# Half-size tiles for weight blocks that are split alone, and three raw weight tiles in place of four

## The chip, the cores and the metric

The kernel runs on one core of a Trainium2 chip. The metric is the device time of one execution in microseconds (us); the time before is the median of 3 runs. The engines are TensorE (PE; its weight loads are PEld), VectorE (DVE), ScalarE (ACT), GpSimd (POOL) and SyncE (SP), which here issues nearly all loads.

## The reference

Two decoder layers on 256 tokens of width 2048, in float32. Each layer has a token mixer (HGRN2 in the first, gated linear attention in the second) that shares an input projection with a cross-attention into 256 memory tokens, an output projection, and a SwiGLU feed-forward of width 5632:

```python
    for layer in range(DEPTH):
        hn = _rmsnorm(h, norm_mix[layer])
        ...
        h = h + jnp.concatenate([y, xa], axis=-1) @ w_out[layer]

        hn = _rmsnorm(h, norm_ffn[layer])
        gate, up = jnp.split(hn @ w_gate_up[layer], 2, axis=-1)
        h = h + (jax.nn.silu(gate) * up) @ w_down[layer]
    return _rmsnorm(h, norm_final)
```

What is left out computes y, the mixer's output, and xa, the cross-attention's. Each weight is read once, so the kernel is a stream of weight tiles through the products.

## The kernel before

**Split weights.** Each float32 operand is taken apart into a high part, rounded to the matmul's fp32r format, and a low part, the rest; a product is then three matmuls: high by high, high by low, low by high. For the weights this happens as they come. A load (on SP's queue, L216 and L341) brings a raw tile of four 128 x 512 blocks, 1 MB. `split` takes one or two blocks of it: ScalarE casts them to the high part (L207) and VectorE subtracts to get the low part (L208); both go into one tile called `parts`. TensorE reads the parts.

**The rings.** Raw tiles come from a ring of four, parts from a ring of six, each with room for two blocks, high and low. A load waits until the last split has read the raw tile whose place it takes; a cast waits until TensorE is done with the parts tile whose place it takes. A few other tiles (`side`: keys and values of the memory, a small decay table) sit in the ring of parts for a while.

**Two ways to multiply.** `project` (mixers, w_out, w_down; L249 to L251) splits a raw tile into two parts tiles and makes 24 matmuls of it. `project_halves` (the gate and up product; L333 to L335) saves products by combining blocks. One raw tile holds two blocks of gate and two of up, comes by two loads of 512 KB (the first brings the block that a splits), and is of one of three kinds:

- O: two splits of two blocks (a, b), 24 matmuls.
- H: as O, then one difference (L366) and a split of one block alone (c), 24 matmuls.
- S: a split of one block alone (a), a split of two (b), then three differences written over the raw tile (L350 on two blocks, L351, L352), then two splits of two (c, d), 21 matmuls. L351 needs L350, L352 needs L351, c needs L350, d needs L352.

So an S tile takes four parts tiles, one of them half full; an H tile takes three, one of them half full.

**The feed-forward's blocks.** Each layer has 11 blocks of 512 columns. A block takes eight gate and up tiles, of kinds SHOSHOSO, SHOSSOSO, SHOSSOSO, and from the fourth block (number 3) on SSOSSOSS; then VectorE and ScalarE combine the eight products into the silu-gated result (L830 to L836), TensorE transposes it (L160, with L148 and L149), and pieces of w_down follow between the blocks: four raw tiles per block from block 3 on, with L414 adding the result to the residual. Blocks 3 to 10 are called steady here. Raw tiles are numbered through: 148 to 155 are the gate and up tiles of block 6 of the first layer (kinds S, S, O, S, S, O, S, S), 156 to 159 the w_down tiles behind them.

**What sets the order.** Nothing in the code fixes the order on an engine. A scheduler takes the instructions in the code's order of priority and places each when its inputs and a free slot of its ring are expected; engines then run their lists strictly in order and wait by semaphores. So ring sizes decide not only who waits, but also the lists.

Of the kernel before, what the change touches and what calls it, by code (L numbers as in the profile page):

```python
# [9 lines left out]
F32 = mybir.dt.float32  # L10
F32R = mybir.dt.float32r
# [6 lines left out]
P = 128  # L18
# [17 lines left out]
def trunk_kernel(ctx: ExitStack, tc: tile.TileContext, x, mem, norm_mix, norm_ffn, norm_mem,  # L36
# [5 lines left out]
    wts = ctx.enter_context(tc.tile_pool(name="wts", bufs=1))  # L42
# [153 lines left out]
    def new_raw():  # L196
        i = n_w[0]
        n_w[0] += 1
        return i, wts.tile([P, 4, 512], F32, tag="raw", name=f"raw{i}", bufs=4)

    def split(src, name, by=2):

        n, m = src.shape[1:]
        both = wts.tile([P, 2, 2, 512], F32R, tag="parts", name=f"parts{name}", bufs=6)
        for k in range(0, n, by):
            j = min(k + by, n)
            nc.scalar.copy(out=both[:, 0, k:j, 0:m], in_=src[:, k:j, :])  # L207
            nc.vector.tensor_tensor(out=both[:, 1, k:j, 0:m], in0=src[:, k:j, :],  # L208
                                    in1=both[:, 0, k:j, 0:m].bitcast(F32), op=ALU.subtract)
        return [(both[:, 0, k, 0:m], both[:, 1, k, 0:m]) for k in range(n)]  # L210

    def weights(w, k0, nk, c0, n):
        i, raw = new_raw()
        m = 1 if i == 0 else nk
        for j in range(0, nk, m):
            nc.sync.dma_start(out=raw[:, j:j + m, 0:n],  # L216
                              in_=w[(k0 + j) * P:(k0 + j + m) * P, c0:c0 + n].rearrange("(k p) c -> p k c", p=P))
        return [p for k in range(0, nk, 2) for p in split(raw[:, k:k + 2, 0:n], f"{i}_{k}", 1 if i == 0 else 2)]
# [102 lines left out]
    def project_halves(forms, kinds, w, c0, c1, name):  # L321
# [14 lines left out]

        for p, kind in enumerate(kinds):
            i, raw = new_raw()

            for j, c in ((slice(0, 4, 3), c0), (slice(1, 3), c1)):  # L340
# [4 lines left out]
            if kind == "S":  # L345
                tt = nc.vector.tensor_tensor
                b00, = split(raw[:, 0:1, :], f"{i}a")
                b11, b10 = split(raw[:, 2:4, :], f"{i}b")

                tt(out=raw[:, 0:2, :], in0=raw[:, 0:4:2, :], in1=raw[:, 1:2, :].broadcast_to([P, 2, 512]), op=ALU.subtract)  # L350
                tt(out=raw[:, 2, :], in0=raw[:, 2, :], in1=raw[:, 0, :], op=ALU.add)  # L351
                tt(out=raw[:, 3, :], in0=raw[:, 3, :], in1=raw[:, 2, :], op=ALU.subtract)  # L352
                t5, t7 = split(raw[:, 0:2, :], f"{i}c")
                t6, t4 = split(raw[:, 2:4, :], f"{i}d")
                todo = {1: ("x00", b00), 2: ("x01", b10), 3: ("z", b11), 4: ("x11", t4), 5: ("s", t5), 6: ("u", t6),
                        7: ("d0", t7)}
                for b in (1, 2, 6, 7, 5, 4, 3) if last else (1, 3, 2, 5, 7, 6, 4):
                    product(b, x(todo[b][0]), todo[b][1])
            else:
                b00, b01 = split(raw[:, 0:2, :], f"{i}a")  # L360
                b11, b10 = split(raw[:, 2:4, :], f"{i}b")
                todo = [[(2, "x00", b00), (5, "x10", b01), (4, "x10", b00), (3, "d0", b01)]]
                if kind == "O":
                    todo.append([(2, "x01", b10), (5, "x11", b11), (4, "x11", b10), (3, "d1", b11)])
                else:
                    nc.vector.tensor_tensor(out=raw[:, 3, :], in0=raw[:, 3, :], in1=raw[:, 2, :], op=ALU.subtract)  # L366
                    e1, = split(raw[:, 3:4, :], f"{i}c")
                    todo.append([(2, "x01", b10), (3, "x01", b11), (7, "x11", b11), (4, "x11", e1)])
                todo = [m for ms in zip(*todo) for m in ms] if last else todo[0] + todo[1]
                for b, f, right in todo:  # L370
                    product(b, x(f), right)
# [586 lines left out]
```

## Time and profile before

| | |
|---|---|
| time, median of 3 runs | 2323.41 us (2322.97 to 2323.65) |
| the profiled execution: time, span | 2322.12 us, 2320.3 us |
| TensorE's granted clock | 0.998 |
| read from memory | 430.48 MB, 187 GB/s over the span |
| blocks 3 to 10, first layer | about 675 to 1170 us |
| blocks 3 to 10, second layer | about 1740 to 2240 us |

How to read the rows that follow: a page line gives busy time, share of the span and instructions per engine. A row of windows has the stretch, its length, then busy time and count of PE, PEld, DVE, ACT and POOL, the granted clock, the share of DMA, and GB/s. A row of the timeline has start, duration, engine, line, operation, output from inputs, shapes, and in brackets how long the engine stood idle ahead of it and what ended that. A matmul's duration reaches into the next one's, since they are pipelined: the distance of starts is what counts, and the same holds, less so, for VectorE and ScalarE. A row of DMA issues has tiles, queue, count, KB of one and the median time from issue to landing.

### The profile page before, as it was taken

The numbers are of one execution on the slowest core, as the hardware profiler recorded it, in microseconds if no ns is written. First come the engines' busy times: TensorE is split into PE (matmuls) and PEld (weight loads), VectorE is DVE, ScalarE is ACT, GpSimd is POOL, SyncE is SP. The second block draws the span as 40 slices with busy tenths as digits, with TensorE's granted clock in tenths as the row PEclk, the third lists the DMA queues.
The fourth block names the chain that finished last, engine by engine and source line by source line (L and its number), as shares of the span: only waits on it lengthen the run. The fifth ranks groups of instructions, "written<-read, shape, count | busy, mean of one in ns | idle before, by whom it ended". The sixth has DMA issues, their size and how long they took to land.

```text
span 2320.3 us, 28901 instructions
## 1 busy us (share of the span) xinstructions
PE 2297.6 (99%) x11034; PEld 1934.7 (83%) x11034; DVE 1887.7 (81%) x2262; ACT 1261.2 (54%) x1643; POOL 22.2 (1%) x39
## 2 busy tenths in 40 slices
PE   9999999999999999999999999999999999999998
PEld 7888888888887888888889999988887888888886
DVE  5566565668999999999985665567999999999995
ACT  7543534455555555555555654455555555555563
POOL 0000000000000000000000000000000000000000
PEclk9999999999999999999999999999999999999999
DMA  8554545455556556566565445555555556656563
GB/s 316 192 172 162 164 150 176 145 182 176 186 188 212 200 188 205 189 209 208 183 226 167 150 150 167 161 199 164 178 203 198 201 187 210 202 189 210 200 217 127
DMA packets 229211, 435.51 MB, mean 188 GB/s; under 512 B 10028, under 2 KB 38992, under 8 KB 228816
## 3 DMA queue, kind: packets, MB, share of 16 engines
q1 hardware_dynamic: 227776, 429.40, 55.5%
q10 hardware_dynamic: 1296, 4.26, 0.5%
q8 instruction: 86, 1.41, 0.2%
q14 instruction: 53, 0.43, 0.1%
HBM read 430.48 MB, written 3.15 MB: 187 GB/s over the span
## 4 chain that ended last, share of the span: by engine, by line
PE 63%; DVE 25%; issue 6%; ACT 4%; DMA 0%; ACTq 0%; DVEq 0%; POOLq 0%; SPq 0%
PE f_p L334 5%; PE f_p L335 5%; PE f_p L333 4%; DVE raw L350 4%; DVE parts L208 4%; PE fd L250 3%; PE fd L249 3%; PE fd L251 3%; PE wo L251 3%; PE wo L249 3%; PE wo L250 3%; DVE raw L351 2%; DVE raw L352 2%; PE hgate L249 1%; PE gv L249 1%
## 5 line engine op out<-in xcount | busy, mean ns | idle before, releaser
L208 DVE TENSOR_TENSOR parts<-raw,parts 128x1024 fp32r<-128x1024 f32 (+3 forms) x490 | 557.7, 1147 | 289.1 <-ACT parts L207 288.2
L207 ACT CAST parts<-raw 128x1024 fp32r<-128x1024 f32 (+3 forms) x490 | 476.8, 991 | 424.6 <-PE wo L251 64.4
L350 DVE TENSOR_TENSOR raw<-raw 128x1024 f32<-128x1024 f32 x118 | 143.6, 1217 | 0.2
L351 DVE TENSOR_TENSOR raw<-raw 128x512 f32<-128x512 f32 x118 | 81.6, 692 | 3.9
L352 DVE TENSOR_TENSOR raw<-raw 128x512 f32<-128x512 f32 x118 | 81.6, 692 | 3.8
L414 DVE TENSOR_TENSOR h<-fd,h 128x512 f32<-128x512 f32 x94 | 61.9, 684 | 6.2 <-PE fd L251 6.1
L833 DVE TENSOR_TENSOR e<-f_p,e 128x512 f32<-128x512 f32 x66 | 44.9, 680 | 0.0
L835 ACT ACTIVATE s<-s,rf_r 128x512 f32<-128x512 f32 x44 | 31.8, 722 | 6.9 <-DVE s L833 6.9
L836 DVE SCALAR_TENSOR_TENSOR s<-e,rf_r,s 128x512 f32<-128x512 f32 x44 | 32.3, 742 | 0.0
L562 DVE COPY_PREDICATED sch<-mask,slh 96x512 f32<-96x512 uint8 (+3 forms) x15 | 10.8, 721 | 25.1 <-PE slh L578 25.1
L833 DVE TENSOR_TENSOR s<-f_p,e 128x512 f32<-128x512 f32 x44 | 29.5, 682 | 0.0
L578 PEld LDWEIGHTS slh<-Q,K 128*96 128x96 f32 (+3 forms) x240 | 25.4, 176 | 1.4
L249 PE MATMUL wo<-parts,y_3h 128*128 128x512 f32 x64 | 25.9, 405 | 0.0
L249 PE MATMUL wo<-parts,y_0h 128*128 128x512 f32 x64 | 25.7, 402 | 0.0
L250 PE MATMUL fd<-parts,s_3h 128*128 128x512 f32 x64 | 25.4, 396 | 0.0
L249 PE MATMUL fd<-parts,s_0h 128*128 128x512 f32 x64 | 25.3, 396 | 0.0
L249 PE MATMUL fd<-parts,s_2h 128*128 128x512 f32 x64 | 25.3, 396 | 0.0
L249 PE MATMUL fd<-parts,s_6h 128*128 128x512 f32 x64 | 25.3, 396 | 0.0
L249 PE MATMUL fd<-parts,s_4h 128*128 128x512 f32 x64 | 25.3, 396 | 0.0
L250 PE MATMUL fd<-parts,s_5h 128*128 128x512 f32 x64 | 25.3, 396 | 0.0
L249 PE MATMUL fd<-parts,s_8h 128*128 128x512 f32 x64 | 25.3, 396 | 0.0
L250 PE MATMUL fd<-parts,s_0h 128*128 128x512 f32 x64 | 25.3, 396 | 0.0
(5486 smaller groups left out, 7396.4 us busy)
## 6 DMA issues: line engine op xcount, KB each, us to landing
raw<-in_w_gate_up_dram SPq DMA_DIRECT2D x352, 512.0 KB, 4.0
raw<-in_w_down_dram SPq DMA_DIRECT2D x88, 1024.0 KB, 5.0
raw<-in_hgrn_w_in_dram SPq DMA_DIRECT2D x52, 1024.0 KB, 5.0
raw<-in_gla_w_in_dram SPq DMA_DIRECT2D x48, 768.0 KB, 4.3
raw<-in_w_out_dram SPq DMA_DIRECT2D x32, 1024.0 KB, 4.9
raw<-in_w_mem_kv_dram SPq DMA_DIRECT2D x15, 1024.0 KB, 8.2
raw<-in_gla_w_in_dram SPq DMA_DIRECT2D x8, 528.0 KB, 3.7
mtok<-in_mem_dram SPq DMA_DIRECT2D x4, 512.0 KB
```

The source lines that it names most:

```text
L207: nc.scalar.copy(out=both[:, 0, k:j, 0:m], in_=src[:, k:j, :])
L208: nc.vector.tensor_tensor(out=both[:, 1, k:j, 0:m], in0=src[:, k:j, :], in1=both[:, 0, k:j, 0:m].bitcast(F32), op=ALU.subtract)
L249: nc.tensor.matmul(acc, xh, hi[:, o:o + m], start=first, stop=False)
L250: nc.tensor.matmul(acc, xh, lo[:, o:o + m], start=False, stop=False)
L251: nc.tensor.matmul(acc, xl, hi[:, o:o + m], start=False, stop=last)
L333: nc.tensor.matmul(ps[b], xh, hi, start=first, stop=False)
L334: nc.tensor.matmul(ps[b], xh, lo, start=False, stop=False)
L335: nc.tensor.matmul(ps[b], xl, hi, start=False, stop=left[b] == 0)
L350: tt(out=raw[:, 0:2, :], in0=raw[:, 0:4:2, :], in1=raw[:, 1:2, :].broadcast_to([P, 2, 512]), op=ALU.subtract)
L351: tt(out=raw[:, 2, :], in0=raw[:, 2, :], in1=raw[:, 0, :], op=ALU.add)
L352: tt(out=raw[:, 3, :], in0=raw[:, 3, :], in1=raw[:, 2, :], op=ALU.subtract)
L833: nc.vector.tensor_tensor(out=out, in0=ps[p], in1=q, op=ALU.add)
```

## The change

Blocks that are split alone (a of an S tile, c of an H tile) get tiles of their own with room for one block, in a ring of two called `part`. The six full tiles stay. The ring of raw tiles has three in place of four: 3 x 8 + 6 x 8 + 2 x 4 = 80 KB per partition, as 4 x 8 + 6 x 8 before.

```diff
--- before.py
+++ after.py
@@ -196,12 +196,15 @@
     def new_raw():
         i = n_w[0]
         n_w[0] += 1
-        return i, wts.tile([P, 4, 512], F32, tag="raw", name=f"raw{i}", bufs=4)
+        return i, wts.tile([P, 4, 512], F32, tag="raw", name=f"raw{i}", bufs=3)
 
     def split(src, name, by=2):
 
         n, m = src.shape[1:]
-        both = wts.tile([P, 2, 2, 512], F32R, tag="parts", name=f"parts{name}", bufs=6)
+        if n == 1:
+            both = wts.tile([P, 2, 1, 512], F32R, tag="part", name=f"parts{name}", bufs=2)
+        else:
+            both = wts.tile([P, 2, 2, 512], F32R, tag="parts", name=f"parts{name}", bufs=6)
         for k in range(0, n, by):
             j = min(k + by, n)
             nc.scalar.copy(out=both[:, 0, k:j, 0:m], in_=src[:, k:j, :])
```

Lines behind this place stand three lower: L207 and L208 become L210 and L211, L350 to L352 become L353 to L355, L414 becomes L417, L830 to L836 become L833 to L839.

No instruction is added or taken away. A raw tile's load now waits for the last split of the tile three before it, where it waited for the one four before; SP's list is the same but for one small load. In the mixers the lists of VectorE and ScalarE are unchanged. In the feed-forward they move, in every steady block alike. In the rows below, the number in a tile's name is the raw tile's (148, 149 and so on), a to d the piece; the last number only tells tiles apart, and fd rows add a w_down result to the residual h.

VectorE, from the end of tile 149 to the start of 151. Before:

```order
L351 TENSOR_TENSOR raw149_6608<-raw149_6608 128x512
L352 TENSOR_TENSOR raw149_6608<-raw149_6608 128x512
L208 TENSOR_TENSOR parts149c_6620<-raw149_6608,parts149c_6620 128x1024
L208 TENSOR_TENSOR parts149d_6623<-raw149_6608,parts149d_6623 128x1024
L208 TENSOR_TENSOR parts150a_6650<-raw150_6647,parts150a_6650 128x1024
L208 TENSOR_TENSOR parts150b_6653<-raw150_6647,parts150b_6653 128x1024
L208 TENSOR_TENSOR parts151a_6683<-raw151_6680,parts151a_6683 128x512
L208 TENSOR_TENSOR parts151b_6686<-raw151_6680,parts151b_6686 128x1024
```

Now, from the last piece of tile 148 on:

```order
L211 TENSOR_TENSOR parts148d_6577<-raw148_6562,parts148d_6577 128x1024
L211 TENSOR_TENSOR parts149b_6614<-raw149_6608,parts149b_6614 128x1024
L211 TENSOR_TENSOR parts149c_6620<-raw149_6608,parts149c_6620 128x1024
L354 TENSOR_TENSOR raw149_6608<-raw149_6608 128x512
L355 TENSOR_TENSOR raw149_6608<-raw149_6608 128x512
L211 TENSOR_TENSOR parts151a_6683<-raw151_6680,parts151a_6683 128x512
L211 TENSOR_TENSOR parts149d_6623<-raw149_6608,parts149d_6623 128x1024
L211 TENSOR_TENSOR parts150a_6650<-raw150_6647,parts150a_6650 128x1024
L211 TENSOR_TENSOR parts150b_6653<-raw150_6647,parts150b_6653 128x1024
L211 TENSOR_TENSOR parts151b_6686<-raw151_6680,parts151b_6686 128x1024
L353 TENSOR_TENSOR raw151_6680<-raw151_6680 128x1024
L211 TENSOR_TENSOR parts152a_6722<-raw152_6719,parts152a_6722 128x512
```

151a has moved ahead of 149d, and 152a between the differences of 151; the load of tile 151 is now set free by 148d, five operations ahead of 151a, and that of 152 by 149d.

VectorE in the middle of tile 148. Before:

```order
L208 TENSOR_TENSOR parts148b_6568<-raw148_6562,parts148b_6568 128x1024
L350 TENSOR_TENSOR raw148_6562<-raw148_6562 128x1024
L351 TENSOR_TENSOR raw148_6562<-raw148_6562 128x512
L352 TENSOR_TENSOR raw148_6562<-raw148_6562 128x512
L208 TENSOR_TENSOR parts148c_6574<-raw148_6562,parts148c_6574 128x1024
L208 TENSOR_TENSOR parts148d_6577<-raw148_6562,parts148d_6577 128x1024
```

Now:

```order
L211 TENSOR_TENSOR parts148b_6568<-raw148_6562,parts148b_6568 128x1024
L353 TENSOR_TENSOR raw148_6562<-raw148_6562 128x1024
L211 TENSOR_TENSOR parts149a_6611<-raw149_6608,parts149a_6611 128x512
L354 TENSOR_TENSOR raw148_6562<-raw148_6562 128x512
L211 TENSOR_TENSOR parts148c_6574<-raw148_6562,parts148c_6574 128x1024
L355 TENSOR_TENSOR raw148_6562<-raw148_6562 128x512
```

The three differences stood in a row; now a piece of this or of the next tile stands between them, and d comes later. Tiles 151 and 154 have the same form as 148, tiles 149 and 152 that of the rows further up.

VectorE at the end of a block, where tile 155 is the last. Before:

```order
L351 TENSOR_TENSOR raw155_6830<-raw155_6830 128x512
L352 TENSOR_TENSOR raw155_6830<-raw155_6830 128x512
L208 TENSOR_TENSOR parts155c_6842<-raw155_6830,parts155c_6842 128x1024
L833 TENSOR_TENSOR s0_6_6870<-f0_6_p2_6588,e0_6_6869 128x512
L208 TENSOR_TENSOR parts155d_6845<-raw155_6830,parts155d_6845 128x1024
L208 TENSOR_TENSOR parts156_0_6887<-raw156_6885,parts156_0_6887 128x1024
```

Now:

```order
L211 TENSOR_TENSOR parts155c_6842<-raw155_6830,parts155c_6842 128x1024
L354 TENSOR_TENSOR raw155_6830<-raw155_6830 128x512
L836 TENSOR_TENSOR s0_6_6870<-f0_6_p2_6588,e0_6_6869 128x512
L355 TENSOR_TENSOR raw155_6830<-raw155_6830 128x512
L211 TENSOR_TENSOR parts155d_6845<-raw155_6830,parts155d_6845 128x1024
L211 TENSOR_TENSOR parts156_0_6887<-raw156_6885,parts156_0_6887 128x1024
```

The last difference (L352, now L355) has moved from ahead of c to right ahead of d. The s0 row is the first step towards the silu's input.

ScalarE at the same place. Before:

```order
L207 CAST parts155c_6842<-raw155_6830 128x1024
L830 COPY e0_6_6869<-f0_6_p1_6580 128x512
L207 CAST parts155d_6845<-raw155_6830 128x1024
L207 CAST parts156_0_6887<-raw156_6885 128x1024
L835 ACTIVATE s0_6_6870<-s0_6_6870,rf0_r_3976 128x512
```

Now:

```order
L210 CAST parts155c_6842<-raw155_6830 128x1024
L833 COPY e0_6_6869<-f0_6_p1_6580 128x512
L838 ACTIVATE s0_6_6870<-s0_6_6870,rf0_r_3976 128x512
L210 CAST parts155d_6845<-raw155_6830 128x1024
L210 CAST parts156_0_6887<-raw156_6885 128x1024
```

The silu (ACTIVATE of s0), which waits for VectorE's s0 row, has moved ahead of the casts of 155d and of the first w_down tile.

## Prediction

> **What bounds the kernel now.** I read the busy times, then windows by stage, then the timeline of one steady feed-forward block.
>
> ```profile
> span 2320.3 us, 28901 instructions
> PE 2297.6 (99%) x11034; PEld 1934.7 (83%) x11034; DVE 1887.7 (81%) x2262; ACT 1261.2 (54%) x1643; POOL 22.2 (1%) x39
> ```
>
> TensorE (PE) looks full everywhere, but its busy time overlaps with itself, so the stages have to be told apart by VectorE (DVE): a window of the first mixer, the early feed-forward blocks, and one steady block (from L350 of its last tile to the same place 12 tiles on).
>
> ```profile
> 280.00:385.00 105.00, 105.00 (x554) 89.47 (x553) 62.57 (x81) 46.76 (x67) 2.92 (x3) 1.00 0.49 161
> ...
> 600.00:650.00 50.00, 49.32 (x222) 40.43 (x221) 48.23 (x55) 28.40 (x33) 0.00 (x0) 1.00 0.57 187
> ...
> 853.16:916.33 63.17, 62.71 (x278) 50.97 (x277) 62.45 (x71) 36.08 (x41) 0.00 (x0) 1.00 0.60 200
> ```
>
> The mixer has VectorE busy 60%: TensorE sets its pace. In the steady block VectorE is busy 62.45 of 63.17 us. TensorE's own need there follows from its start times, 55 starts apart:
>
> ```profile
> 936.81 0.39 PE L250 MATMUL fd<-parts,s_3h 128*128 128x512 f32 x1
> 949.28 0.39 PE L335 MATMUL f_p<-parts160d,hf_0l 128*128 128x512 f32 x1
> ```
>
> 12.47/55 = 0.227 us each. A steady block has six S tiles of 21, two O tiles and four w_down tiles of 24: 270 x 0.227 = 61.2 us, and eight transposes, about 0.7: 61.9. So VectorE's 63.15 bounds the block, and TensorE has 1.2 us to spare. How many such blocks there are: the same instruction in blocks 3 and 10 of each layer.
>
> ```profile
> 726.57 1.22 DVE L350 TENSOR_TENSOR raw<-raw 128x1024 f32<-128x1024 f32 x1
> 1168.95 1.22 DVE L350 TENSOR_TENSOR raw<-raw 128x1024 f32<-128x1024 f32 x1
> ...
> 1795.71 1.22 DVE L350 TENSOR_TENSOR raw<-raw 128x1024 f32<-128x1024 f32 x1
> 2238.13 1.22 DVE L350 TENSOR_TENSOR raw<-raw 128x1024 f32<-128x1024 f32 x1
> ```
>
> 442.4/7 = 63.2 us in both. With block 3 itself, 2 x 8 = 16 blocks run so.
>
> **What VectorE does in an S tile.** Here tile 149, then an O tile and the start of 151:
>
> ```profile
> 884.80 1.22 DVE L350 TENSOR_TENSOR raw<-raw 128x1024 f32<-128x1024 f32 x1
> 886.05 0.69 DVE L351 TENSOR_TENSOR raw<-raw 128x512 f32<-128x512 f32 x1
> 886.78 0.69 DVE L352 TENSOR_TENSOR raw<-raw 128x512 f32<-128x512 f32 x1
> 887.39 1.22 DVE L208 TENSOR_TENSOR parts149c<-raw,parts149c 128x1024 fp32r<-128x1024 f32 x1
> 888.66 1.22 DVE L208 TENSOR_TENSOR parts149d<-raw,parts149d 128x1024 fp32r<-128x1024 f32 x1
> 889.80 1.22 DVE L208 TENSOR_TENSOR parts150a<-raw,parts150a 128x1024 fp32r<-128x1024 f32 x1
> 890.94 1.22 DVE L208 TENSOR_TENSOR parts150b<-raw,parts150b 128x1024 fp32r<-128x1024 f32 x1
> 892.08 0.68 DVE L208 TENSOR_TENSOR parts151a<-raw,parts151a 128x512 fp32r<-128x512 f32 x1
> ```
>
> Start to start, a 1024-wide operation that depends on nothing near takes 1.14 us (149d to 150a). L350 to its dependent L351 takes 1.25, L351 to L352 0.73 against 0.61, c to d 1.27 against 1.14. So each S tile has pauses of 0.11 + 0.12 + 0.13 us; in a block's last tile an L833 fills the third. Per block: 6 x 0.23 + 5 x 0.13 = 2.03 us.
>
> **The change, part by part.**
>
> *The pauses that go.* In the new order L350 is nearly always parted from L351, and L351 mostly from L352. That such a pair, once parted, loses its pause is seen in the first block:
>
> ```profile
> 566.28 1.23 DVE L350 TENSOR_TENSOR raw<-raw 128x1024 f32<-128x1024 f32 x1
> 567.42 1.22 DVE L208 TENSOR_TENSOR parts90b<-raw,parts90b 128x1024 fp32r<-128x1024 f32 x1
> 568.67 0.69 DVE L351 TENSOR_TENSOR raw<-raw 128x512 f32<-128x512 f32 x1
> 569.28 1.22 DVE L208 TENSOR_TENSOR parts90c<-raw,parts90c 128x1024 fp32r<-128x1024 f32 x1
> 570.42 0.68 DVE L352 TENSOR_TENSOR raw<-raw 128x512 f32<-128x512 f32 x1
> 572.29 1.23 DVE L208 TENSOR_TENSOR parts90d<-raw,parts90d 128x1024 fp32r<-128x1024 f32 x1 [1.20 <-ACT parts90d L207]
> ```
>
> L350 to 90b takes 1.14, L351 to 90c 0.61. What stays per block: L351 to L352 in tiles 149 and 152 (0.24), and about 0.13 before each of 151d and 154d, which have one 1024-wide operation between L352 and themselves. Gain 2.03 - 0.50 = 1.53 us.
>
> The Trainium skill, page VectorE: DVE Perf Modes, section The DRAIN you can't avoid, says that a semaphore between two VectorE operations costs nothing extra. By it 1.25 against 1.14 would not come from the wait, and parting the pair would gain nothing; the rows above disagree, and I go by them.
>
> *d right behind L352.* The last two rows show the price: ScalarE can cast d only after L352, so d starts 1.87 us after L352 instead of 0.60: 1.27 us lost. Before, c stood between them. In the new order the last tile of every block has L355 (the old L352) directly ahead of d, and ScalarE has moved its silu ahead of that cast, which frees it, by L836 on VectorE, about when L355 would. Cost 1.27 us a block, whatever the loads do. TensorE waits behind d too, but has the slack.
>
> *A load that comes late.* With three raw tiles, tile 151's load waits for 148d (before: 147's last operation). The new order puts 151a five operations behind 148d; 154a behind 151d likewise. The load in rows: issue and time to landing of the first half of a gate_up load (it holds what a needs), the time to landing of one issued 2.3 us behind another (after 150b), and that of all gate_up and w_down loads of the first layer's feed-forward.
>
> ```profile
> 889.91 0.88 SPq L341 DMA_DIRECT2D raw<-in_w_gate_up_dram  x2
> ...
> DMA to landing us min/median/max: 3.6/3.6/3.6
> ...
> DMA to landing us min/median/max: 4.6/4.6/4.6
> ...
> DMA to landing us min/median/max: 3.6/4.5/5.9
> ```
>
> The cast: one that waited for a w_down load, which was issued 5.06 us earlier and takes 5.0 to land by its group's row; and two in succession.
>
> ```profile
> 858.72 0.37 SPq L216 DMA_DIRECT2D raw<-in_w_down_dram  x1
> ```
>
> ```profile
> 863.78 1.05 ACT L207 CAST parts<-raw 128x1024 fp32r<-128x1024 f32 x1 [0.51 <-DMA raw<-in_w_down_dram]
> ...
> 890.44 0.61 ACT L207 CAST parts151a<-raw 128x512 fp32r<-128x512 f32 x1
> 890.95 1.05 ACT L207 CAST parts151b<-raw 128x1024 fp32r<-128x1024 f32 x1
> ```
>
> ```profile
> raw<-in_w_down_dram SPq DMA_DIRECT2D x88, 1024.0 KB, 5.0
> ```
>
> Count from the start of 148d. The issue follows 1.25 us later (149d at 888.66, issue 889.91), landing 3.6 on, the cast's start 0.1 on, and VectorE may begin 0.65 after that (0.61 for the cast and a little for the signal): 5.6 us. VectorE arrives after 148d, 149b, 149c, L354, L355: 3 x 1.14 + 0.73 + 0.61 = 4.76. It waits 0.85 us. Queued behind are 149d, 150a, 150b, 151b; on ScalarE the cast of 149d stands behind that of 151a, so it begins at 5.5 and VectorE's 149d at 6.55 instead of 6.2: 0.35 more. Together 1.2 us, twice a block: 2.4. The casts of 152a and 155a come out even: their loads are set free by 149d and 152d, and four operations of 1.14 us follow (with d itself 5.7 us against 5.6). Bounds: if the load cost nothing, 149d would still wait for its cast, 1.27 less the 0.6 of 151a: 0.67 a place. If every first half took 4.6, each place costs 2.2, and 152a and 155a 0.9 each. I take 3.6, since nothing else is in flight on that queue then, as at 889.91. The Trainium skill, page DMA: Bandwidth & Descriptors, section Anatomy of one DMA, fits 2.0 us plus bytes/436 GB/s, made for another issuing path; for 512 KB that is an estimate of 3.2 us against the measured 3.6, and the whole sum would be about 21 us instead of 34.
>
> *Three raw tiles elsewhere.* In the mixers ScalarE's two casts per tile follow TensorE 2.72 us apart:
>
> ```profile
> 45.65 1.06 ACT L207 CAST parts<-raw 128x1024 fp32r<-128x1024 f32 x1 [1.66 <-PE mv L251]
> 48.37 1.05 ACT L207 CAST parts<-raw 128x1024 fp32r<-128x1024 f32 x1 [1.66 <-PE mv L251]
> ...
> raw<-in_hgrn_w_in_dram SPq DMA_DIRECT2D x52, 1024.0 KB, 5.0
> ```
>
> A tile takes 5.44 us, so a load freed two tiles ahead has some 10 us for its 5.0: nothing, with half of that cover left. Order on VectorE and ScalarE is unchanged there. At the start loads are bandwidth-bound, and their bytes stay: 0, at worst +3 us. Blocks 0 to 2 of each layer have both engines near full (600 to 650 above); blocks 1 and 2 get one late load and lose some pauses: 0, between -1 and +2 us each.
>
> *More parts tiles.* An S tile takes three full slots instead of four. That frees only ScalarE's waits for TensorE, which VectorE doesn't feel in the steady block (0.7 us idle in all): 0.
>
> *Sum.* Per steady block: 2.4 + 1.27 - 1.53 = +2.1 us, to 65.3; 16 blocks: +34 us. The profiled execution took 2322.1 us (span 2320.3), 1.3 below the median of the runs: 2356 for it, 2357 for the median.
>
> **Rivals.**
> 1. *Loads cost nothing* (they land before VectorE arrives): 2 x 0.67 + 1.27 - 1.53 = +1.1 a block, +17 us: 2340. For it: ScalarE is only half busy; against it, 3.6 us is the shortest landing in the row over the whole feed-forward. Chance 0.13.
> 2. *Loads queue up* at 4.6 us: 4.4 + 1.8 + 1.27 - 1.53 = +5.9 a block, +95 us: 2418. For it, the 4.6 row; against it, the loads in question are over 6 us behind the one ahead. 0.12.
> 3. *Pauses stay* though their pairs are parted: only the c-to-d part is then saved (5 x 0.13 - 0.26 = 0.39), +3.3 a block, +52 us: 2375. The 566.28 and 568.67 rows speak against it. 0.04. The Trainium skill's section cited above (VectorE: DVE Perf Modes) would have it so.
> 4. *Faster:* the deeper ring of split tiles lets ScalarE cast so far ahead that VectorE never waits; TensorE's 61.9 us then bounds the block, -1.2 x 16 = -19 us: 2304. It decides once the new waits fall under 1.5 us a block. Against it: the 1.27 us behind L355 is a data dependence that no slot removes. 0.06.
> 5. *No change:* waits and saved pauses cancel, 2323. 0.05.
>
> My own forecast keeps 0.60. A difference under 0.2% (4.6 us) is what a measurement here can't tell from none. Slower: 0.60 + 0.13 + 0.12 + 0.04 = 0.89; same 0.05; faster 0.06. The range of 2336 to 2390 reaches from rival 1 past rival 3 and leaves out rivals 4 and 5 and most of rival 2.
>
> **What would show it.** Steady blocks of about 65.3 us between the same instructions; VectorE idle about 3.9 us a block, put down to ScalarE's casts: near 0.85 ahead of 151a and 154a, 0.35 ahead of 149d and 152d, 1.27 ahead of 155d; 1.14 us from L353 to what follows; the load of 151 issued as 148d ends; mixers unchanged. The forecast is wrong if first halves land under 3 us or over 4.2, if L836 waits for TensorE at a block's end, or if the mixers stretch.

## The result and the profile after

The changed kernel takes 2361.78 us (median of 4 runs, 2360.44 to 2364.30) against 2323.19 for the kernel before: 1.0168 times as long, 95% interval 1.0154 to 1.0182. It is slower by 38.6 us. Busy times barely move, on the page of the changed kernel:

```profile
span 2360.2 us, 28789 instructions
...
PE 2314.1 (98%) x11034; PEld 1929.3 (82%) x11034; DVE 1877.3 (80%) x2262; ACT 1261.0 (53%) x1643; POOL 22.2 (1%) x39
```

VectorE does the same 2262 instructions in a little less busy time. What grew is the time between them, and only in one stage. The windows of the changed kernel: the mixer and the early blocks as in the prediction, then seven steady blocks of the first layer (from 119b to 203b on VectorE), then one of them (143d to 155d).

```profile
280.00:385.00 105.00, 105.00 (x554) 89.49 (x553) 62.63 (x82) 46.77 (x67) 2.92 (x3) 1.00 0.48 161
600.00:650.00 50.00, 49.80 (x224) 40.98 (x223) 46.78 (x54) 26.59 (x32) 0.00 (x0) 1.00 0.57 191
729.39:1190.90 461.51, 448.57 (x1948) 355.32 (x1946) 433.22 (x485) 252.70 (x288) 0.00 (x0) 1.00 0.57 192
866.67:932.69 66.02, 64.10 (x278) 50.75 (x278) 61.88 (x69) 36.05 (x42) 0.00 (x0) 1.00 0.58 191
```

The mixer's row is that of before. Seven steady blocks take 461.5 us instead of 442.4: 65.9 a block against 63.2. (In the second layer 459.4: 65.6.) VectorE is busy 61.88 of 66.02 us in the block, where it was 62.45 of 63.17. Where it stands idle, the view of waits for VectorE, in the window of this one block, tells:

```profile
DVE parts155d L211 <- ACT parts155d L210: 1.2, 1, 1.2
DVE parts154a L211 <- ACT parts154a L210: 1.0, 1, 1.0
DVE parts151a L211 <- ACT parts151a L210: 0.9, 1, 0.9
DVE parts155a L211 <- ACT parts155a L210: 0.4, 1, 0.4
DVE parts149d L211 <- ACT parts149d L210: 0.3, 1, 0.3
DVE parts152d L211 <- ACT parts152d L210: 0.3, 1, 0.3
```

(Columns: engine, tile and line that waited, what ended the wait, us in all, times, longest. The view's row for 143d is left out, since it belongs to the block ahead.) All six name ScalarE's cast, but the cast itself was late for two different reasons. At 151a it was the load. Three views of the changed kernel at this place: VectorE, SyncE's queue (its row joins the four issues that follow each other), ScalarE.

```profile
892.43 1.22 DVE L211 TENSOR_TENSOR parts148d<-raw,parts148d 128x1024 fp32r<-128x1024 f32 x1
...
896.55 0.69 DVE L355 TENSOR_TENSOR raw<-raw 128x512 f32<-128x512 f32 x1
898.15 0.69 DVE L211 TENSOR_TENSOR parts151a<-raw,parts151a 128x512 fp32r<-128x512 f32 x1 [0.91 <-ACT parts151a L210]
899.11 1.23 DVE L211 TENSOR_TENSOR parts149d<-raw,parts149d 128x1024 fp32r<-128x1024 f32 x1 [0.27 <-ACT parts149d L210]
```

```profile
893.67 7.57 SPq L344 DMA_DIRECT2D raw<-in_w_gate_up_dram  x4
```

```profile
897.50 0.62 ACT L210 CAST parts151a<-raw 128x512 fp32r<-128x512 f32 x1 [4.26 <-DMA raw<-in_w_gate_up_dram]
898.03 1.05 ACT L210 CAST parts149d<-raw 128x1024 fp32r<-128x1024 f32 x1
```

148d ends, the load of tile 151 is issued at 893.67, the cast of 151a starts 3.83 us later, ScalarE having done nothing for 4.26, and the cast of 149d stands behind it. At the block's end it is the data:

```profile
930.84 0.68 DVE L355 TENSOR_TENSOR raw<-raw 128x512 f32<-128x512 f32 x1
932.69 1.23 DVE L211 TENSOR_TENSOR parts155d<-raw,parts155d 128x1024 fp32r<-128x1024 f32 x1 [1.17 <-ACT parts155d L210]
```

ScalarE can cast d only after L355, so VectorE starts d 1.85 us after L355 instead of 0.60.

### The profile page after: what moved, and what is told of

It is laid out like the page before. It is cut to its first block, busy times and chain, and to the rows that moved or that the text cites. A ratio compares the mean times of both kernels' runs of the same rounds, so it can differ in the third digit from the quotient of the medians.

```text
span 2360.2 us, 28789 instructions
## 1 busy us (share of the span) xinstructions
PE 2314.1 (98%) x11034; PEld 1929.3 (82%) x11034; DVE 1877.3 (80%) x2262; ACT 1261.0 (53%) x1643; POOL 22.2 (1%) x39
## 3 DMA queue, kind: packets, MB, share of 16 engines
q10 hardware_dynamic: 1296, 4.26, 0.5%
## 4 chain that ended last, share of the span: by engine, by line
PE 58%; DVE 22%; DMA 10%; ACT 5%; issue 4%; ACTq 0%; POOLq 0%; SPq 0%; DVEq 0%
DMA raw<-in_w_gate_up_dram 9%; DVE parts L211 4%; PE fd L252 3%; PE fd L253 3%; PE fd L254 3%; PE f_p L337 3%; PE f_p L338 3%; PE f_p L336 3%; PE wo L254 2%; PE wo L252 2%; PE wo L253 2%; DMA raw<-in_w_down_dram 1%; DVE raw L353 1%; DVE raw L354 1%; DVE raw L355 1%
## 5 line engine op out<-in xcount | busy, mean ns | idle before, releaser
L211 DVE TENSOR_TENSOR parts<-raw,parts 128x1024 fp32r<-128x1024 f32 (+3 forms) x490 | 557.7, 1148 | 285.5 <-ACT parts L210 284.7
L210 ACT CAST parts<-raw 128x1024 fp32r<-128x1024 f32 (+3 forms) x490 | 475.7, 990 | 461.0 <-DMA raw<-in_w_down_dram 67.9
L353 DVE TENSOR_TENSOR raw<-raw 128x1024 f32<-128x1024 f32 x118 | 143.8, 1218 | 0.1
L355 DVE TENSOR_TENSOR raw<-raw 128x512 f32<-128x512 f32 x118 | 81.1, 687 | 1.6
L354 DVE TENSOR_TENSOR raw<-raw 128x512 f32<-128x512 f32 x118 | 80.8, 685 | 0.4
L417 DVE TENSOR_TENSOR h<-fd,h 128x512 f32<-128x512 f32 x94 | 60.9, 682 | 10.3 <-PE fd L254 10.3
L836 DVE TENSOR_TENSOR e<-f_p,e 128x512 f32<-128x512 f32 x66 | 45.1, 683 | 0.0
L839 DVE SCALAR_TENSOR_TENSOR s<-e,rf_r,s 128x512 f32<-128x512 f32 x44 | 32.4, 744 | 0.0
L836 DVE TENSOR_TENSOR s<-f_p,e 128x512 f32<-128x512 f32 x44 | 30.0, 685 | 0.1
L252 PE MATMUL fd<-parts,s_7h 128*128 128x512 f32 x64 | 24.8, 397 | 0.9 <-ACT parts L210 0.9
L252 PE MATMUL fd<-parts,s_1h 128*128 128x512 f32 x64 | 24.7, 396 | 0.9 <-ACT parts L210 0.9
```

The costliest lines, as they stand in the source:

```text
L252: nc.tensor.matmul(acc, xh, hi[:, o:o + m], start=first, stop=False)
L836: nc.vector.tensor_tensor(out=out, in0=ps[p], in1=q, op=ALU.add)
```

## The experiments

Two theories stand against each other. Mine: neither three raw tiles nor half tiles cost anything by themselves; they make the scheduler write another order on VectorE and ScalarE, and in that order VectorE waits. The rival: the counts cost (fewer loads ahead, fewer places). To tell them apart, the order has to be held while the counts change, and the counts while the order changes. An order is held with edges between instructions of one engine, which need no semaphore; the order of before, or of after, is written out by tile (0 to 7) and piece, X, Y, Z being the three differences (L353, L354, L355):

```diff
+    vec = {}
+    def in_order(names):
+        for one, two in zip(names, names[1:]):
+            tc.add_manual_dep(vec[two], vec[one].name, mybir.DependencyInfo(
+                mybir.DependencyClass.NoSync, mybir.DependencyReason.DATA), reason="order")
...
+            if b >= 3:
+                in_order([f"{n0 + int(k[0])}{k[1]}" for k in SEQ])
+                in_order([f"h{n0 + int(k[0])}{k[1]}" for k in ACT_SEQ])
```

`vec` holds the instruction of each split and of each difference. SEQ is VectorE's order, ACT_SEQ that of ScalarE's casts. Everything else is left to the scheduler. All times stand beside runs of the kernel before on the same chip (2322.7 to 2323.2 us); "a block" is the mean of seven steady blocks of the first layer. In the table, the order "before" is held by the list of old_order, or is the scheduler's own, which has the splits and differences in the same order; "after" is held by the list of new_order_4raw.

| run | raw / full / half | order | us | ratio to before (95%) | a block |
|---|---|---|---|---|---|
| before | 4 / 6 / - | before | 2323.2 | | 63.2 |
| after | 3 / 6 / 2 | after | 2361.8 | 1.0168 (1.0154 to 1.0182) | 65.9 |
| three_raw | 3 / 6 / - | before | 2323.06 | 1.0001 (0.9991 to 1.0010) | 63.2 |
| old_order | 3 / 6 / 2 | before | 2320.74 | 0.9992 (0.9982 to 1.0001) | 63.2 |
| new_order_4raw | 4 / 5 / 2 | after | 2336.94 | 1.0061 (1.0046 to 1.0076) | 64.3 |
| new_end | 3 / 6 / 2 | after, but for the end | 2346.74 | 1.0103 (1.0087 to 1.0118) | 65.0 |
| second_half_first | 3 / 6 / 2 | after | 2453.12 | 1.0558 (1.0543 to 1.0574) | 71.5 |
| first_row_alone | 3 / 6 / 2 | after | 2335.53 | 1.0052 (1.0035 to 1.0068) | 64.5 |
| half_tiles_4_5_2 | 4 / 5 / 2 | scheduler's | 2351.81 | 1.0126 (1.0111 to 1.0141) | 65.4 |
| old_order_L353_early | 3 / 6 / 2 | before, X ahead of b | 2331.75 | 1.0038 (1.0024 to 1.0053) | 63.8 |
| written_order_4_6 | 4 / 6 / - | written | 2333.34 | 1.0043 (1.0028 to 1.0058) | 63.9 |
| written_order_4_5_2 | 4 / 5 / 2 | written | 2324.47 | 1.0007 (0.9998 to 1.0016) | 63.5 |
| written_order_in_turn | 4 / 5 / 2 | written, products in turn | 2302.46 | 0.9913 (0.9898 to 0.9928) | 61.9 |
| in_turn_4_6 | 4 / 6 / - | written, products in turn | 2307.23 | 0.9933 (0.9916 to 0.9951) | 62.1 |

**Three raw tiles alone.** The kernel before with one number changed; the scheduler gives the splits and differences of the weights in the order of before.

```diff
-        return i, wts.tile([P, 4, 512], F32, tag="raw", name=f"raw{i}", bufs=4)
+        return i, wts.tile([P, 4, 512], F32, tag="raw", name=f"raw{i}", bufs=3)
```

> The kernel before with three raw tiles in place of four and nothing else; the order on VectorE and ScalarE stays as before. My theory (the cost comes from the order that the tile counts bring about): in that order tile 151's load is freed by 148d and seven operations, about 7 us and more, stand between that and 151a, against 3.7 us of landing: no wait, 63.2 us a steady block, 2323 us within 3. Rival (three raw tiles by themselves, or what they do to the loads, cost the 39 us): 2355 to 2365. In between would mean that half of it is the ring.

Measured: 2323.06 us, no difference. Its seven blocks:

```profile
726.60:1169.30 442.70, 440.78 (x1947) 358.08 (x1947) 437.13 (x485) 252.77 (x287) 0.00 (x0) 1.00 0.60 200
```

So a load that starts a tile later is not felt where nine splits and differences (I had written seven) stand between what sets it free and the piece that needs it, nor in the mixers.

**All of the change, but the order of before.**

```diff
+    SEQ = "0a 0b 0X 0Y 0Z 0c 0d 1a 1b 1X 1Y 1Z 1c 1d 2a 2b 3a 3b 3X 3Y 3Z 3c 3d ... 7a 7b 7X 7Y 7Z 7c 7d".split()
+    ACT_SEQ = "0a 0b 0c 0d 1a 1b 1c 1d 2a 2b 3a 3b 3c 3d ... 7a 7b 7c 7d".split()
```

> The changed kernel with the same tile counts (three raw, six full, two half), but in the steady blocks (3 to 10 of each layer) VectorE's and ScalarE's operations on the weights are held in the order of before. My theory: all of the loss goes, 63.2 us a steady block, 2323 us within 4 (perhaps 1 to 3 under it, since blocks 0 to 2 keep the new order and had gained). Rival (the counts cost by themselves, whatever the order): stays at 2355 to 2365.

Measured: 2320.74 us, the whole loss gone with every tile count as in the changed kernel. This decides it for the order: in the order of before, the counts cost nothing. The 2.2 us under before are at the edge of what can be told.

**The order of after, with loads early.** Four raw tiles and five full ones, so that the bytes stay; the order of after held.

```diff
-        return i, wts.tile([P, 4, 512], F32, tag="raw", name=f"raw{i}", bufs=3)
+        return i, wts.tile([P, 4, 512], F32, tag="raw", name=f"raw{i}", bufs=4)
...
-            both = wts.tile([P, 2, 2, 512], F32R, tag="parts", name=f"parts{name}", bufs=6)
+            both = wts.tile([P, 2, 2, 512], F32R, tag="parts", name=f"parts{name}", bufs=5)
...
+    SEQ = "0a 0b 0X 1a 0Y 0c 0Z 1X 0d 1b 1c 1Y 1Z 3a 1d 2a 2b 3b 3X 4a 3Y 3c 3Z 4X 3d 4b 4c 4Y 4Z 6a 4d 5a 5b 6b 6X 7a 6Y 6c 6Z 7X 6d 7b 7c 7Y 7Z 7d".split()
+    ACT_SEQ = "0a 0b 1a 0c 0d 1b 1c 3a 1d 2a 2b 3b 4a 3c 3d 4b 4c 6a 4d 5a 5b 6b 7a 6c 6d 7b 7c 7d".split()
```

(The lines are set against the changed kernel; `side`, which shares the ring of parts, goes from six to five with it.)

> Four raw tiles, five full, two half (the same bytes), and in the steady blocks VectorE's and ScalarE's operations on the weights held in the order of the changed kernel: the loads are early again, the rest of the order stays. My theory: the waits for a late load go (151a, 154a, 155a), and what the order costs by itself stays: 0.65 us ahead of 149d and of 152d, 1.27 ahead of 155d, less 1.5 of saved pauses: +1.1 us a block, 64.3 us, 2340 us in all (2334 to 2346). Rival 1 (the late loads are all of the loss): 2323 or less. Rival 2 (the order is all of the loss, the loads don't matter): 2355 to 2365.

Measured: 2336.94 us, 64.3 a block, as worked out. The same place as above, in this run:

```profile
889.69 0.69 DVE L362 TENSOR_TENSOR raw<-raw 128x512 f32<-128x512 f32 x1
890.30 0.68 DVE L218 TENSOR_TENSOR parts151a<-raw,parts151a 128x512 fp32r<-128x512 f32 x1
891.58 1.22 DVE L218 TENSOR_TENSOR parts149d<-raw,parts149d 128x1024 fp32r<-128x1024 f32 x1 [0.59 <-ACT parts149d L217]
```

(L362 is L355 here.) 151a no longer waits, and 149d waits 0.6 us for its own cast, which the late load had half covered. Of the 38.6 us, early loads give back about 25 (with one full tile fewer); what the order costs by itself is the other 14. So three raw tiles are free in the order of before and not in this one.

**Another end of the block.** The order of after, but at the end of each block that of before.

```diff
-    SEQ = "... 7X 6d 7b 7c 7Y 7Z 7d".split()
+    SEQ = "... 7X 6d 7b 7Y 7Z 7c 7d".split()
```

> The changed kernel with its own order in the steady blocks held as it was, but for each block's end: 155b, L354, L355, 155c, 155d instead of 155b, 155c, L354, L355, 155d, so that 155c and a silu operation stand between L355 and 155d as before. My theory: the 1.25 us ahead of 155d go and a pause of 0.12 between L354 and L355 comes in: about -1.1 us a block, 64.8 us, 2343 us (2340 to 2348). Rival (the time at a block's end is only taken there because VectorE is ahead; it turns up as another wait in the next block): 2358 to 2362.

Measured: 2346.74 us, 1.0 us a block less. The time does not come back elsewhere, so the rival falls. I had said 1.1, and the rest stands in the rows: L361 (the second difference) now follows b at once, and loses 0.12 us there too.

```profile
924.08 1.22 DVE L218 TENSOR_TENSOR parts155b<-raw,parts155b 128x1024 fp32r<-128x1024 f32 x1
925.34 0.69 DVE L361 TENSOR_TENSOR raw<-raw 128x512 f32<-128x512 f32 x1
926.06 0.69 DVE L362 TENSOR_TENSOR raw<-raw 128x512 f32<-128x512 f32 x1
```

**The landing, later and sooner.** Two kernels with counts and order of after, which differ only in how the 1 MB of a gate and up tile is fetched. The first turns its two loads round, so that a's row comes with the second:

```diff
-            for j, c in ((slice(0, 4, 3), c0), (slice(1, 3), c1)):
+            for j, c in ((slice(1, 3), c1), (slice(0, 4, 3), c0)):
```

> The changed kernel, orders on VectorE and ScalarE held as they are, but of each gate_up tile's two loads the one without a's row is issued first, so that a's row comes with the second. My theory (a wait ahead of 151a, 154a, 155a is for the landing of a's half): the landing that a needs goes from 3.8 to about 4.6 us after the issue, so 0.8 us more ahead of 151a, 154a and 155a each and 0.75 ahead of 152a: +3.2 a block, 69.2 us, 2412 us (2400 to 2420). Rival (VectorE waits there for a place in a ring or for ScalarE, not for the load): 2358 to 2366.

The second fetches a's row by itself, ahead of the rest:

```diff
+            for j, r, c in ((0, 0, c0), (slice(1, 3), slice(0, 2), c1), (3, 1, c0)):
+                rows = w[2 * p * P:(2 * p + 2) * P, c:c + 512].rearrange("(k p) c -> p k c", p=P)
+                nc.sync.dma_start(out=raw[:, j, :], in_=rows[:, r, :])
```

> The changed kernel, orders held as they are, but a's row (256 KB) is loaded by itself first, then the two rows of the other half, then the fourth: three loads in place of two, the same bytes. My theory: the waits ahead of 151a, 154a and 155a (1.0, 1.0, 0.5 us) fall by what the smaller load lands sooner than 3.8 us; at 3.3 us that is 0.5 + 0.5 + 0.5 a block, 24 us in all: 2338 (if it lands no sooner: 2362; under 2.8 us: 2325 to 2330). The waits ahead of 149d, 152d and 155d stay within 0.1. Rival (three issues in place of two put the later loads back and cost more than is won): over 2362.

Measured: 2453.12 and 2335.53 us. The place of 151a in the kernel with the halves turned round, SyncE's queue and ScalarE:

```profile
907.73 8.81 SPq L351 DMA_DIRECT2D raw<-in_w_gate_up_dram  x4
```

```profile
912.80 0.62 ACT L217 CAST parts151a<-raw 128x512 fp32r<-128x512 f32 x1 [5.50 <-DMA raw<-in_w_gate_up_dram]
```

and in the kernel that loads the first row alone:

```profile
886.63 1.32 SPq L352 DMA_DIRECT2D raw<-in_w_gate_up_dram  x3
```

```profile
889.40 0.63 ACT L217 CAST parts151a<-raw 128x512 fp32r<-128x512 f32 x1 [3.21 <-PE f_p L345]
890.24 1.05 ACT L217 CAST parts149d<-raw 128x1024 fp32r<-128x1024 f32 x1 [0.21 <-DVE raw L362]
```

From issue to cast it is 5.07 us with the halves turned round, 3.83 in the changed kernel and 2.77 with the first row alone; in the last the cast was released by TensorE, who gave the half tile's place free, so the load had landed by then. The waits ahead of 151a, 154a and 155a are gone with the first row alone but for two places in the first layer (166a 1.3 us, 199a 1.6), and what is left is nearly what the run with four raw tiles had left (64.5 and 64.3 a block). For a landing under 2.8 us I had said 2325 to 2330; it is 2335.5, because 149d and 152d, which I had put within 0.1 us of the changed kernel, now wait 0.5 in place of 0.26: as with four raw tiles, no earlier wait covers theirs any more. With the halves turned round they grow by 1.2 to 1.4 us at each of the four places where an a comes early (in the mean of the steady blocks of the first layer, 151a waits 2.4, 154a 2.2, 152a 1.5 and 155a 1.3). The direction is as expected, but I had taken 0.8 us for what the landing would lose, from a pair of loads in the kernel before, and it lost 1.24; so the time came out 41 us over the forecast of this run. Both runs show that VectorE waits there for the landing of a's row.

**Half tiles alone.** Four raw tiles kept, five full and two half, and the order left to the scheduler (its list for tiles 0 to 7 follows).

```
0a 0b 0X 1a 0Y 0c 0Z 1X 0d 1b 1c 1Y 3a 1Z 3X 4a 1d 2a 2b 3b 3c 3Y 4X 3Z 6a 3d 4b 4c 4Y 6X 4Z 7a 7X 4d 5a 5b 6b 6c 6Y 6Z 6d 7b 7c 7Y 7Z 7d
```

> The other half of the change alone: half tiles (two), four raw tiles kept, five full ones in place of six (the same bytes), and the order left to the scheduler. It comes out as another order again: 151a and 152a ahead of 149d, 154a and one L351-type operation ahead of 151d, and in tiles 154 and 155 d directly (154) or with nothing but a pause (155) behind L352-type. My theory (cost read from the order): 0.65 us ahead of 151d, 1.25 ahead of 154d, 1.25 ahead of 155d, pauses saved 1.8: +1.4 a block, 64.5 us, 2345 us (2336 to 2350). Rival (it takes both halves of the change, that is late loads, to lose): 2323 or less.

Measured: 2351.81 us, slower, just over my range. Both d's right behind their Z cost what they should:

```profile
920.27 0.69 DVE L355 TENSOR_TENSOR raw<-raw 128x512 f32<-128x512 f32 x1
922.16 1.23 DVE L211 TENSOR_TENSOR parts154d<-raw,parts154d 128x1024 fp32r<-128x1024 f32 x1 [1.20 <-ACT parts154d L210]
```

What I missed is 6a (tile 154): its load is set free by 2b, five operations stand between the two, and it waits 0.3 to 1.9 us, 1.05 in the mean of eight blocks, for the landing. So a late load doesn't need three raw tiles; it needs an order that asks early.

**What a pause is.** The order of before, but X ahead of b, so that b parts X from Y.

```diff
-    SEQ = "0a 0b 0X 0Y 0Z 0c 0d 1a 1b 1X ...".split()
+    SEQ = "0a 0X 0b 0Y 0Z 0c 0d 1a 1X 1b ...".split()
```

> As old_order (the counts of the change, the order of before), but L353-type (the first difference) stands ahead of b in place of behind it, so that b parts it from the second difference. My theory: one pause of 0.11 us goes per S tile, six a block: 62.5 us, 10 us under old_order: 2310 us (2308 to 2313). Rival 1 (a pause comes from any operation of the tile just ahead, so b in its place brings the same pause): 2321. Rival 2 (TensorE, not VectorE, holds the block at 63.2): 2318 to 2321.

Measured: 2331.75 us, neither my 2310 nor the rival's 2321, but 11 us slower than old_order. The rows say why (L360 is X, L361 Y, L362 Z):

```profile
886.30 0.68 DVE L218 TENSOR_TENSOR parts149a<-raw,parts149a 128x512 fp32r<-128x512 f32 x1
887.02 1.23 DVE L360 TENSOR_TENSOR raw<-raw 128x1024 f32<-128x1024 f32 x1
888.16 1.22 DVE L218 TENSOR_TENSOR parts149b<-raw,parts149b 128x1024 fp32r<-128x1024 f32 x1
889.41 0.69 DVE L361 TENSOR_TENSOR raw<-raw 128x512 f32<-128x512 f32 x1
```

X to b takes 1.14 us: no pause, b needs nothing of X. But a to X takes 0.72 instead of 0.61, since X overwrites the block that a has just read, and b to Y 1.25 instead of 1.14, since Y overwrites what b reads. Two pauses have taken the place of one: 0.11 x 6 = 0.66 us a block, 10.6 in 16 blocks, against 11.0 measured. Here a pause comes from overwriting what the operation just ahead reads as well as from reading what it wrote.

**An order written out.** With that, an order can be made in which, as far as the rows so far tell, VectorE need not wait: a of the next tile between X and Y, c between Y and Z, the next tile's X and b between Z and d. The first two runs wrote it for the counts of before and for 4 / 5 / 2.

```diff
+    SEQ = "0a 0b 0X 1a 0Y 0c 0Z 1X 1b 0d 1Y 1c 1Z 2a 2b 1d 3a 3b 3X 4a 3Y 3c 3Z 4X 4b 3d 4Y 4c 4Z 5a 5b 4d 6a 6b 6X 7a 6Y 6c 6Z 7X 7b 7Y 6d 7Z 7c 7d".split()
```

Here the code itself emits the splits in this order, and the products of a tile behind its last piece. In both, one factor of an O tile's products is x10 in place of x00, so the sums that they form are not the layer's; the operations, their number and their shapes are the same.

> The tile counts of before (four raw, six full, no half), and in the steady blocks an order on VectorE and ScalarE that is written out: in S tiles of a pair L350, a of the next, L351, c, L352, then the next tile's L350 and b before d; so every dependent pair is parted, d has 1.3 us or more of other work behind L352, and c to d too. My theory (VectorE's time in a steady block is its operations plus what its order makes it wait): pauses of 2.0 us a block go and nothing comes in, VectorE would need 61.2 and TensorE's 61.9 becomes the bound: 2303 to 2312. Rival (d comes to TensorE 1.1 us later than in the old order, and the pieces of the next tile hold ring places meanwhile, so TensorE and ScalarE wait instead): 2320 to 2335.

> The same written order with four raw, five full and two half tiles. My theory: as with six full tiles, 2303 to 2314; an S tile now takes three full places of five instead of four of six, which is about the same lead. Rival (five places are too few, casts wait for TensorE and VectorE for them): over 2323.

Measured: 2333.34 us, slower than before, and 2324.47, no difference; both lie where the rivals had them. VectorE had lost its pauses, but with five full places it waited for the casts of 151b and 154b (0.6 and 0.7 us a block), and with six for those of 151b, 151c, 154b and 154c (0.5 to 0.8 each). In block 6, the casts of 151b and 154b had themselves waited 1.9 to 2.0 us for TensorE to give a place free. The order had a flaw: an O tile's last piece stands ahead of the d before it, so its 24 products had moved ahead of that S tile's 21 on TensorE, and places of the ring came free late. The next run puts the products in the order of the tiles.

> The written order with four raw, five full and two half tiles as in the run of that name, but TensorE's products stand in the order of the tiles (there, those of an O tile stood ahead of those of the S tile before it), and the operand that was exchanged there is right. My theory: the waits of 154b and 151b for ScalarE's casts, 0.6 us each a block, were for ring places that TensorE gave free late; with them gone VectorE needs 62 us and TensorE's 62 is the bound: 62.2 to 62.8 a block, 2305 to 2314 us. Rival (what holds the 63.4 us there is TensorE itself): 2318 to 2325.

Measured: 2302.46 us, a little under my range, faster than before by 0.87% (0.72 to 1.02), and than the changed kernel by 59 us. The casts of 151b and 154b no longer wait for TensorE, nor VectorE for them. Its seven blocks:

```profile
722.30:1155.70 433.40, 433.40 (x1936) 357.13 (x1935) 430.04 (x485) 257.07 (x288) 0.00 (x0) 1.00 0.61 204
```

TensorE is busy all the time, 61.9 us a block; there is nothing left for VectorE to give. The last run asks whether half tiles have a part in it.

> The order of written_order_in_turn with the tile counts of before: four raw, six full, no half tiles, so that a takes a full place too. It tells whether half tiles are worth anything once the order is written out. My theory (they are, in this order: 3c and 6c need the place of the O tile's first half, which TensorE gives free some 5 us after 1d, 4d): 0.5 to 1.3 us of wait ahead of 151c, 154c or the b behind them, 62.9 to 64 a block, 2315 to 2335 us. Rival (six full places do as well; the gain is the order's alone): 2300 to 2306.

Measured: 2307.23 us, 62.1 a block. My theory falls: with the tile counts of before the same order gives 16 of the 20 us. Half tiles, with one full tile fewer, add 4.8 us, 0.2%, at the limit of what can be told.

## Why the prediction was right, and where it was short

The prediction said 2357 us within 2336 to 2390, slower by late loads and by d right behind L355, less some pauses. It measured 2361.8, and each step can be held against a run.

- *The pauses that go*: right. L353 to the operation that parts it takes 1.14 us in the changed kernel:

```profile
885.94 1.21 DVE L353 TENSOR_TENSOR raw<-raw 128x1024 f32<-128x1024 f32 x1
887.08 0.68 DVE L211 TENSOR_TENSOR parts149a<-raw,parts149a 128x512 fp32r<-128x512 f32 x1
```

  The 0.13 us between c and d, which the prediction counts among the pauses, is of another kind: d needs nothing of c, and in its rows of tile 149 d starts 1.88 us behind L352 with c in between, as it does with nothing in between (1.87 in tile 90). It is what is left of the way over ScalarE. The size was right all the same.
- *d right behind L352* (L355 after): 1.27 forecast, 1.25 in the rows of 155d. Undoing it alone gave back 1.0 a block, because the new place brought pauses of its own.
- *A load that comes late*: the mechanism is right to the instruction, as the two runs with other loads show. This is the term that was mis-sized. The step "I take 3.6" makes 3.7 us from issue to cast; in block 6 it took 3.83 for 151a and 3.88 for 154a, which waited 0.99 and 1.04 us instead of 0.85 (149d and 152d 0.36 and 0.35, as forecast). Over the eight blocks of the first layer VectorE stands idle 8.7 us ahead of the 151a's and 7.8 ahead of the 154a's, 1.09 and 0.97 a block; in the second layer it is 0.93 and 0.84, and the layers' blocks take 65.9 and 65.6 us for the 65.3 forecast. 152a and 155a, which were to come out even, nearly do: in the first layer 155a waits in block 6 alone (0.47 us, issue to cast 4.26 there) and 152a's like in block 3 alone (116a, 0.7).
- *Three raw tiles elsewhere*: right. Mixers are unchanged. TensorE's first product of the first layer's block 1 (tile 92) starts 0.95 us later than before, that of block 2 (102) 0.4, that of block 3 (112) 2.2, all within the ranges given; from there to the end of the feed-forward the delay grows by 20.7 us, and in the second layer by 17.9: 38.6 in the 16 steady blocks of the profiled executions, for the 34 forecast.
- *More parts tiles*: 0, right for the counts (old_order), but only with the order told apart from them. Left to the scheduler, half tiles with four raw and five full ones cost 29 us.
- *Rivals*: that loads cost nothing would have given 64.3 a block and 2340; taking the late loads away (new_order_4raw) gave 64.3 and 2337, so its terms were right and its condition was not met. That pauses stay though their pairs are parted is refuted by the rows. The faster rival, TensorE's 61.9 us as the bound and 2304 in all, isn't what the change does, but it is what the written order reached: 61.9 and 2302. The 1.27 us behind L355, which "no slot removes", an order removes.

## What to carry to other kernels

Where a scheduler writes the instruction lists, ring sizes can change the order as well as the buffering, and the two work on each other: here three raw tiles cost nothing in the old order and about 25 us in the new one, which cost 14 more by itself. Compare the lists before and after, and hold the order fixed to find out which of the two costs. On an engine that sets the pace, go through its list pair by pair: put something between an operation and the next one that reads its result or overwrites its input, put more than the other engine's time between an operation and the piece that must pass through that engine, and more than a landing between what frees a buffer and what needs its next load. When such a list is written out, keep the consumer's order as it was, since the consumer frees the places.

## What was not expected of the hardware

- A VectorE operation that overwrites what the one just ahead has read starts 0.11 us later than one that doesn't (0.72 for 0.61, 1.25 for 1.14), as much as one that reads what the one ahead wrote. The Trainium skill, page VectorE: DVE Perf Modes, section The DRAIN you can't avoid, has a semaphore between two VectorE operations cost nothing extra, measured on eight copies in a row. Here a wait for something long done costs nothing either (149b needs ScalarE's cast and starts 1.14 us behind X), but a wait for the operation just ahead costs 0.11; the rows decide, and the time of a whole kernel (11 us for one pause more in each of 96 S tiles) goes with them.
- Of two 512 KB loads issued one behind the other, data of the second reached ScalarE 5.07 us after the first issue, data of the first 3.83; of a 256 KB load issued ahead, within 2.77. The 1.24 us cost 5.6 us a block, since four pieces then waited where two had (5.2 of the 5.6 stand ahead of these four); the 1.06 us gave back 1.4, where early loads (four raw tiles) gave 1.6.
- With the halves turned round, the granted clock in the steady blocks was 0.97 (row below), against 1.00 in every other run; TensorE paused most there (two of its starts lay up to 2.6 us apart, 1.7 in the changed kernel). Whether the pauses made it was not tried.

```profile
732.70:1233.10 500.40, 467.65 (x1947) 363.41 (x1946) 433.78 (x484) 250.37 (x288) 0.00 (x0) 0.97 0.53 177
```
